# Four more seven-product units in the gate and up projections of a one-core encoder layer

## The chip, the core and the metric

The kernel runs on one core of a Trainium2 chip. The metric is the device time of one launch in microseconds. The core's engines work side by side: PE (TensorE, matrix products into PSUM), DVE (VectorE), ACT (ScalarE), POOL (GpSimd; here it issues DMAs, above all those that add into their target) and SP (SyncE; it issues most DMAs). Each takes its own instructions strictly in order.

## The reference, cut to what matters

One encoder layer over 256 tokens of width 2048: a mixing part (input projection, windowed attention, a gated recurrence, output projection), a gated feed-forward part and a gated per-layer embedding, all in fp32. The change is in the feed-forward part:

```python
fn = rms_norm(h, g_ffn_pre)                                  # 256 x 2048
ff = (silu(fn @ w_ffn_gate) * (fn @ w_ffn_up)) @ w_ffn_down  # 2048 -> 5632 -> 2048
h  = h + rms_norm(ff, g_ffn_post)
```

## The kernel before

**Tiles.** Weights come from memory in tiles of 128 partitions x 2 x 512 (512 KB): two neighbouring blocks of 128 rows, 512 columns. Every fp32 operand is split into a high part (`wh`, made by a cast on ACT at L681) and a low part (`wl` = tile minus high part, on DVE at L697); one product of a 128x128 activation block with a 128x512 weight block is then three matmuls (high-high, low-high, high-low). PE can't begin a tile before its cast, nor the third matmul on it before its low part.

**Steps.** The gate and up projections go in eleven steps f = 0 to 10, each 512 columns of both; three groups of steps (0 to 3, 4 to 7, 8 to 10) are each followed by two down steps that multiply the finished columns by `w_ffn_down`. A step takes eight *units*: one pair of row blocks (kx = 0, 2, ... 14) for both matrices, against both halves of the tokens. A plain unit is a 2x2 by 2x2 block product of eight products, 24 matmuls, on two weight tiles (L735 to L737).

**Seven-product units.** For the units kx = 0, 2, 4 of steps 2 to 10 the eight products are replaced by seven (21 matmuls, L746 to L748), as in Strassen's and Winograd's scheme. The price is paid in sums. On the side of the activations four sums `S1, S2, S7, S4` per unit are made once for all steps by `sums_of` (L847, L854, and a split at L318 and L320); their scratch space is a part of the tile `ple`, and the sums for kx = 4 go to a tile `s`. On the side of the weights each unit of each step needs three sums of 128x512 on DVE (L625, L627, L631) from the gate tile and the up tile, and one that a DMA from POOL adds in place (L650). The unit's up tile, its *second tile*, is kept from its load until late, in one of five places (`lower`, `lower2`, a part of `ple`) that are handed out in turn.

A unit's tiles are used in this order. First the *four*: four products on two tiles of sums, issued while PE is still on the step ahead. When all fours of a step are done, `made_of_four` (L794 to L803: an ACT copy, four DVE operations, an ACT copy) combines the four accumulators, and the rest of the step waits for this. Then come the plain units, between them the *two* of each unit (its kept second tile), and last the *one* (one tile for up to two units). The tables `TAKEN` and `FOURS` say after which plain unit each comes, by the kind of step: `up3` is a gate-up step with three seven-product units, `up0` one without, `down4` a down step with four.

**Order.** Everything is written in an order that a planner in the kernel makes: it holds an estimated clock per engine, costs per operation, due times and priorities (`plan.add(task, ready, late)`), and records the operations as its clocks let them start. A task added with a later ready time stands later in the queues of its engines.

**Between steps.** A step's output `mid` is transposed by DVE (L346) and sixteen small DMAs (L356, `mT<-mid`, by POOL, or half by POOL and half by SP in the last step of a group), and then cast and split for the down steps (`carried`: L318 on ACT, L320 on DVE). Partial sums of the down steps are parked in memory; the last of them come back as `mg<-part`, 1 MB for each half of the tokens (L1914, `reload`), in step 10.

Of the kernel before, what the change touches and what calls it, by code (L numbers as in the profile page):

```python
# [16 lines left out]
P = 128  # L17
# [10 lines left out]
N = 512  # L28
# [14 lines left out]
RING = 5  # L43
# [4 lines left out]
SEVEN_F = range(2, 11)  # L48

SWAPPED = [  # L50
    (lambda f: (("w_ffn_gate", f), ("w_ffn_up", f)), SEVEN_F, SEVEN_KS),
# [196 lines left out]
def layer(ctx: ExitStack, tc: tile.TileContext, a: dict, out: bass.AP):  # L248
# [211 lines left out]
    class Group:  # L460
# [50 lines left out]
        def issue(self, nxt):  # L511
# [16 lines left out]
            for i, k in enumerate(self.rest[:m]):  # L528
# [4 lines left out]
                take()  # L533
            for ch, w, n0 in self.chunks if self.apart else ():
                seg(ch, w, n0, self.lhs, self.rest[m:], first=False)
# [3 lines left out]
    TAKEN = {  # L539
        "up3": ("", "01", "2ab"), "down4": ("", "ab0", "12", "3"), "down2": ("", "01", "a"),  # L540
    }
    FOURS = {
        ("up0", "up3"): (3, 5, 7), ("up3", "up3"): (2, 3, 4), ("up3", "down4"): (2, 3, 3, 4),
# [63 lines left out]
    def sum_stream():  # L607

        for i in sorted(fours):
            at_end = i in ends_with  # L610
            for e in () if at_end else fours[i][4].values():
                yield e
# [11 lines left out]
            both = last_blocks(2)[:, 2 * j : 2 * j + 2, :] if at_end else blocks()[:, b0 : b + 1 : b - b0, :]  # L624
            nc.vector.tensor_tensor(out=both[:, 0, :], in0=Q[:, 0, :], in1=Q[:, 1, :], op=ALU.add)  # L625
            yield dve(N, take=None if at_end else f"t{j}")
            nc.vector.tensor_tensor(out=both[:, 1, :], in0=both[:, 0, :], in1=R[:, 1, :], op=ALU.add)  # L627
# [8 lines left out]
    ends_with, ends_in = {}, {}  # L636

# [121 lines left out]
    def four_products(group, j, i):  # L759
# [9 lines left out]
        product(C2.accs[0], s["S1"], i, 0, first, last)  # L769
        product(C2.accs[1], s["S2"], i, 1, first, last)  # L770
# [36 lines left out]
    def two_products(group, j, i):  # L807
# [10 lines left out]
        if i == mg1_end:  # L818
            plan.add(reload("mg", 0), plan.clk["pe"] + 15.0)
            plan.add(reload("mg", 1), plan.clk["pe"] + 23.0)  # L820
# [9 lines left out]
    def sums_of(lhs, kx, hi, lo):  # L830
# [7 lines left out]
        kind = "mid" if lhs is hP else "T4"  # L838
        for j in range(2):
            h, l = lhs.at[kx + j]  # L840
            yield dve(S, take=None if j else kind)
            if not j and lhs is hP:
# [20 lines left out]
    def more_sums():  # L863
# [5 lines left out]
        for e in hF.ev_sums.values():  # L869
            yield e  # L870
        for j in range(4):
            plan.free[f"t{j}"].append(plan.now)

# [929 lines left out]
    def up_post(f, mid, kk0, g, soon):  # L1803

        def post(ch):
# [13 lines left out]
            plan.add(carried(mid, kk0, mT), plan.now + (0.5 if soon else {0: 12.0, 9: 6.0}.get(f, 3.0)), -SOON if soon else 0.0)  # L1819
# [121 lines left out]
    for part, (f0, f1) in enumerate(PARTS):  # L1941
        mid = Mid(f"mid{part}")
        last_part = part == len(PARTS) - 1
        for f in range(f0, f1):
# [5 lines left out]
                SEVEN_KS if f in SEVEN_F else (),  # L1950
# [226 lines left out]
    for i in range(min(fours), max(f[1] for f in fours.values() if f[4] is hF.ev_sums)):  # L2177
        if i % (W_BUFS + MORE_W) < MORE_W:
            more_w[i] = i % (W_BUFS + MORE_W)
    for n, i in enumerate(sorted(lower)):  # L2180
        lower[i] = (3, 4, 0, 1, 2)[n % RING] if n < len(lower) - 2 else n + 2 - len(lower)
# [144 lines left out]
```

## Time and profile before

| | |
|---|---|
| median of 3 runs | 1143.84 us (1143.76 to 1143.87) |
| the profiled execution | 1142.69 us, span 1140.9 us, clock 0.997 |
| PE busy | 1132.0 us, 5155 instructions |
| DVE busy | 944.0 us |
| ACT busy | 732.1 us |
| POOL busy | 150.1 us |
| step 1 (396.0 to 439.5 us) | DVE busy 33.97 us of 43.5 |
| step 4 (604.5 to 646.0 us) | DVE busy 33.15 us of 41.5 |
| step 8 (852.0 to 893.5 us) | DVE busy 34.83 us of 41.5 |

All times of the trace count from the start of the span. A matmul's row lasts longer than the distance to the next one, since matmuls overlap; the distance between starts is what PE takes for one. In a row of the timeline the bracket at the end gives the idle time of the engine before the row, and what ended it.

### The profile page before, as it was taken

The page shows a single profiled execution, that of the slowest core. Times are in us where ns is not written, and L with a number is a line of the kernel's source. Part 1 is how long each engine was busy: PE and PEld are TensorE (multiplying, and loading weights), DVE is VectorE, ACT ScalarE, POOL GpSimd, SP SyncE. Part 2 cuts the span into 40 slices and gives each one's busy share as a digit, 9 for nine tenths or more (in the row PEclk, how much of TensorE's full clock was granted, in tenths as well). Part 3 has the DMA queues.
Part 4 walks back from the last instruction along what each step waited for, and adds up shares of the span by engine and source line. Part 5 has one row for each costly group of instructions (what it writes and reads, how often), then busy time and mean ns, then how long its engine had stood idle before and what let it go on. Part 6 is the DMA issues. An engine that isn't in the chain of part 4 may idle for free.

```text
span 1140.9 us, 15192 instructions
## 1 busy us (share of the span) xinstructions
PE 1132.0 (99%) x5155; PEld 940.4 (82%) x5155; DVE 944.0 (83%) x1218; ACT 732.1 (64%) x985; POOL 150.1 (13%) x240
## 2 busy tenths in 40 slices
PE   9999999999999999999999999999999999999997
PEld 7888888888888888888888888888888888888886
DVE  5768788788458778898997898999988888888886
ACT  6876788976447555666666566556564565576674
POOL 0000000000000033142110133222111313100200
PEclk9999999999999999999999999999999999999998
DMA  9867576565786996887987777897897777977863
GB/s 311 297 196 222 167 196 194 156 192 187 220 289 185 285 316 208 233 244 224 283 255 218 259 224 216 249 269 247 253 315 247 225 247 239 277 236 256 259 202 105
DMA packets 109967, 268.24 MB, mean 235 GB/s; under 512 B 36352, under 2 KB 42496, under 8 KB 108480
## 3 DMA queue, kind: packets, MB, share of 16 engines
q1 hardware_dynamic: 95568, 242.60, 64.2%
q0 software_dynamic: 14032, 24.52, 10.8%
q8 instruction: 40, 0.66, 0.2%
q14 instruction: 39, 0.32, 0.1%
q10 hardware_dynamic: 288, 0.14, 0.0%
HBM read 249.38 MB, written 9.44 MB: 227 GB/s over the span
## 4 chain that ended last, share of the span: by engine, by line
PE 97%; DMA 1%; DVE 1%; ACT 1%; issue 0%; DVEq 0%; SPq 0%; POOL 0%; ACTq 0%; POOLq 0%
PE acc L737 24%; PE acc L735 24%; PE acc L736 24%; PE acc L748 7%; PE acc L747 7%; PE acc L746 7%; PE tr L337 1%; DMA mg<-part 1%; DVE wl L697 0%; PE half L2044 0%; PE acc L2044 0%; PE warm L2227 0%; PE pg L384 0%; PE pg L385 0%; PE pg L386 0%; DMA mT<-mid 0%
## 5 line engine op out<-in xcount | busy, mean ns | idle before, releaser
L697 DVE TENSOR_TENSOR wl<-wr,wh 128x1024 fp32r<-128x1024 f32 (+1 forms) x300 | 359.2, 1209 | 96.8 <-ACT wh L681 92.1
L681 ACT CAST wh<-wr 128x1024 fp32r<-128x1024 f32 (+1 forms) x300 | 310.5, 1043 | 173.1 <-PE acc L736 115.0
L356 POOL DMA_DIRECT2D mT<-mid x164 | 96.3, 597 | 599.8 <-DMA wr<-in_w_ffn_gate 395.5
L735 PE MATMUL acc<-wh,hT_mix_hi 128*128 128x512 f32 x420 | 163.7, 390 | 0.0
L736 PE MATMUL acc<-wh,hT_mix_lo 128*128 128x512 f32 x420 | 163.5, 389 | 0.0
L737 PE MATMUL acc<-wl,hT_mix_hi 128*128 128x512 f32 x420 | 163.4, 389 | 0.0
L737 PE MATMUL acc<-wl,hT_hi 128*128 128x512 f32 x320 | 124.8, 391 | 0.0
L735 PE MATMUL acc<-wh,hT_hi 128*128 128x512 f32 x316 | 124.5, 394 | 0.0
L736 PE MATMUL acc<-wh,hT_lo 128*128 128x512 f32 x316 | 123.2, 390 | 0.0
L681 ACT CAST wh<-ple 128x1024 fp32r<-128x1024 f32 (+1 forms) x68 | 68.2, 1008 | 75.3 <-DVE ple L627 46.7
L736 PEld LDWEIGHTS acc<-wh,hT_mix_lo 128*128 128x128 f32 x420 | 78.9, 188 | 16.6 <-DVE hT_mix_lo L326 0.3
L737 PEld LDWEIGHTS acc<-wl,hT_mix_hi 128*128 128x128 f32 x420 | 78.8, 188 | 16.4
L735 PEld LDWEIGHTS acc<-wh,hT_mix_hi 128*128 128x128 f32 x420 | 78.8, 188 | 16.3 <-ACT hT_mix_hi L324 0.2
L697 DVE TENSOR_TENSOR wl<-ple,wh 128x1024 fp32r<-128x1024 f32 (+1 forms) x68 | 79.2, 1165 | 10.1 <-ACT wh L681 9.7
L737 PEld LDWEIGHTS acc<-wl,hT_hi 128*128 128x128 f32 x320 | 60.1, 188 | 13.5 <-DVE wl L697 0.6
L736 PEld LDWEIGHTS acc<-wh,hT_lo 128*128 128x128 f32 x316 | 59.4, 188 | 11.8
L735 PEld LDWEIGHTS acc<-wh,hT_hi 128*128 128x128 f32 x316 | 59.4, 188 | 11.3
L650 POOL DMA_DIRECT2D ple<-in_w_ffn_up x27 | 24.1, 891 | 167.7 <-DVE wl L697 125.1
L681 ACT CAST wh<-third 128x1024 fp32r<-128x1024 f32 x33 | 34.7, 1053 | 14.1 <-PE acc L736 8.2
L697 DVE TENSOR_TENSOR wl<-third,wh 128x1024 fp32r<-128x1024 f32 x33 | 40.2, 1220 | 0.7 <-ACT wh L681 0.5
L681 ACT CAST wh<-lower 128x1024 fp32r<-128x1024 f32 x30 | 31.4, 1051 | 13.8 <-PE acc L736 12.1
L735 PE MATMUL acc<-wh,hT_ffn_hi 128*128 128x512 f32 x96 | 37.8, 393 | 0.3 <-ACT hT_ffn_hi L324 0.3
(462 smaller groups left out, 2470.5 us busy)
## 6 DMA issues: line engine op xcount, KB each, us to landing
wr<-in_w_in SPq DMA_DIRECT2D x77, 512.0 KB, 4.4
wr<-in_w_ffn_gate SPq DMA_DIRECT2D x73, 512.0 KB, 5.4
wr<-in_w_ffn_down SPq DMA_DIRECT2D x55, 512.0 KB, 5.5
wr<-in_w_ffn_up SPq DMA_DIRECT2D x51, 512.0 KB, 4.8
wr<-in_w_out SPq DMA_DIRECT2D x32, 512.0 KB, 4.3
wr<-in_w_ple_gate SPq DMA_DIRECT2D x30, 512.0 KB, 5.3
lower<-in_w_ffn_up SPq DMA_DIRECT2D x21, 512.0 KB, 6.2
lower<-in_w_ffn_down SPq DMA_DIRECT2D x17, 512.0 KB, 5.4
```

Of the source, the lines that this page charges most:

```text
L337: nc.tensor.transpose(tr[:, b, t * P : (t + 1) * P], e[:, t, sl], ident)
L356: (nc.gpsimd if i in pool else nc.sync).dma_start(dst[32 * j : 32 * j + 32, :, :, i, :], src[32 * i : 32 * i + 32, :, :, j, :],)
L650: nc.gpsimd.dma_start(dst, src, accum_op=ALU.add)
L681: nc.scalar.copy(his[i][:, 0 : src.shape[1], :] if n == 2 else his[i][:, j, :], src)
L697: nc.vector.tensor_tensor(out=los[i][:, m, :], in0=src, in1=f32(his[i][:, m, :]), op=ALU.subtract)
L735: nc.tensor.matmul(accs[t], hi[:, sl], his[i][:, j, :], start=st, stop=False, **group)
L736: nc.tensor.matmul(accs[t], lo[:, sl], his[i][:, j, :], start=False, stop=False, **group)
L737: nc.tensor.matmul(accs[t], hi[:, sl], los[i][:, j, :], start=False, stop=sp, **group)
L746: nc.tensor.matmul(dst, x[0], wh, start=start, stop=False, skip_group_check=seeded)
L747: nc.tensor.matmul(dst, x[1], wh, start=False, stop=False, skip_group_check=seeded)
L748: nc.tensor.matmul(dst, x[0], wl, start=False, stop=stop, skip_group_check=seeded)
```

## The change

The seven-product scheme takes four more units: in step 1 the units kx = 0 and 2 (a new kind of step, `up2`), and in steps 4 and 8 also kx = 6 (kind `up4`). What comes with it:

- Step 1's two fours stand ahead of the last plain unit of step 0 (`("up0", "up2"): (7, 7)`), so that the sums for kx = 4, which must be out of the shared scratch space before any weight sum uses it, are made earlier too.
- The activation sums for kx = 6 are made later by a new task `fourth_sums`, in a `mid` tile, into a new tile `fourth`. To make room for it, `dynamic_dma_scratch_size=8192` sets the space for the descriptors of the DMAs that POOL issues; before it was left at its default.
- The places of the second tiles are handed out by longest unused, in the rotation 3, 4, 0, 1, 2, with places 0 to 2 for the last four. `flip` swaps the two blocks of a fourth unit's sums where their places would otherwise be in falling order.
- In step 10 the second half of the parked sums is planned 28 us after PE instead of 23, and the last gate-up output of each group is planned for its cast and split 2.5 us after its transposing DMAs instead of 0.5.

```diff
-RING = 5
+RING = (3, 4, 0, 1, 2)
...
-SEVEN_F = range(2, 11)
+SEVEN_F = range(1, 11)
+FOUR_F = (4, 8)
+
+
+def seven_ks(f):
+    return (0, 2, 4, 6) if f in FOUR_F else (0, 2) if f == 1 else SEVEN_KS
...
+            for j, at in enumerate(FOURS[self.kind(), nxt.kind()] if nxt and nxt.sevens else ()):
+                if at >= n:
+                    nxt.four(j)
...
     TAKEN = {
+        "up2": ("", "0", "1a"),
+        "up4": ("", "ab0", "1", "23"),
         "up3": ("", "01", "2ab"), "down4": ("", "ab0", "12", "3"), "down2": ("", "01", "a"),
     }
     FOURS = {
+        ("up0", "up2"): (7, 7), ("up2", "up3"): (2, 3, 4),
+        ("up3", "up4"): (2, 3, 3, 4), ("up4", "up3"): (1, 2, 3), ...
...
-            for e in () if at_end else fours[i][4].values():
-                yield e
+            for e in () if at_end else fours[i][4].items():
+                if e[0] != 6 or fours[i][4] is not hF.ev_sums or fours[i][2] == 3:
+                    yield e[1]
...
+    def flip(i, j):
+        return int(i not in ends_with and j == 3 and first_slot[i] == 0)
...
-            plan.add(reload("mg", 1), plan.clk["pe"] + 23.0)
+            plan.add(reload("mg", 1), plan.clk["pe"] + 28.0)
...
-        kind = "mid" if lhs is hP else "T4"
+        kind = "mid" if lhs is hP or kx == 6 else "T4"
...
+        plan.add(fourth_sums(), plan.now + 20.0, LATE)
+
+    def fourth_sums():
+        pair = t2["pool"].tile([P, 2, N], F32R, name="fourth")
+        yield from sums_of(hF, 6, pair[:, 0, :], pair[:, 1, :])
...
-            plan.add(carried(mid, kk0, mT), plan.now + (0.5 if soon else {0: 12.0, 9: 6.0}.get(f, 3.0)), -SOON if soon else 0.0)
+            plan.add(carried(mid, kk0, mT), plan.now + (2.5 if soon else {0: 12.0, 9: 6.0}.get(f, 3.0)), -SOON if soon else 0.0)
...
-                SEVEN_KS if f in SEVEN_F else (),
+                seven_ks(f) if f in SEVEN_F else (),
...
-        lower[i] = (3, 4, 0, 1, 2)[n % RING] if n < len(lower) - 2 else n + 2 - len(lower)
+        lower[i] = next(j for j in places if j < 3 or n < len(lower) - 4)
+        places.remove(lower[i])
+        places.append(lower[i])
...
-    nc = bacc.Bacc("TRN2", target_bir_lowering=False, num_devices=1)
+    nc = bacc.Bacc("TRN2", target_bir_lowering=False, num_devices=1, dynamic_dma_scratch_size=8192)
```

PE's program falls from 5144 to 5132 instructions, DVE's rises from 1218 to 1246, ACT's from 930 to 938 and POOL's from 245 to 249; SP has 567 in both. Up to the fourteenth weight tile of step 0 the order is the same on every engine. In the rows below, a line number of the changed kernel is 6 to 24 higher than that of the same statement before: L715 is L697, L326 is L320, L332 is L326, L866 is L847, L873 is L854, L640, L642 and L646 are L625, L627 and L631, L699 is L681, L324 is L318, L362 is L356, L584 is L571 and L1938 is L1914.

**DVE at the end of step 0.** `hT_mix_lo` is the low part of the activations' last four blocks, `s` the activation sums for kx = 4, `ple<-wr` and the rows like it weight sums. Before, in the order of the program:

```order
L326 SCALAR_TENSOR_TENSOR hT_mix_lo<-mT,vec,hT_mix_hi 128x256 x4
L847 TENSOR_TENSOR ple<-hT_mix_hi,hT_mix_lo 128x256
L697 TENSOR_TENSOR wl<-wr,wh 128x1024
L847 TENSOR_TENSOR ple<-hT_mix_hi,hT_mix_lo 128x256
L697 TENSOR_TENSOR wl<-wr,wh 128x1024
L854 TENSOR_TENSOR ple<-ple 128x128
L697 TENSOR_TENSOR wl<-wr,wh 128x1024
L854 TENSOR_TENSOR ple<-ple 128x128
L697 TENSOR_TENSOR wl<-wr,wh 128x1024
```

And now, from the same row on:

```order
L332 SCALAR_TENSOR_TENSOR hT_mix_lo<-mT,vec,hT_mix_hi 128x256 x4
L866 TENSOR_TENSOR ple<-hT_mix_hi,hT_mix_lo 128x256 x2
L873 TENSOR_TENSOR ple<-ple 128x128 x4
L326 TENSOR_TENSOR s<-ple,s 128x512
L640 TENSOR_TENSOR ple<-wr 128x512
L642 TENSOR_TENSOR ple<-ple,lower_3577 128x512
L646 TENSOR_TENSOR wr<-wr,lower_3577 128x512
L640 TENSOR_TENSOR ple<-wr 128x512
L715 TENSOR_TENSOR wl<-ple,wh 128x1024
L642 TENSOR_TENSOR ple<-ple,lower_3577 128x512
L715 TENSOR_TENSOR wl<-wr,wh 128x1024
L646 TENSOR_TENSOR wr<-wr,lower_3577 128x512
```

The next three rows are `w<-ple,w`, and `wl<-wr,wh` three times. The low parts of four tiles stood between the activation sums; now the sums for kx = 4 and four of the six weight sums of step 1 stand together ahead of the first low part of step 1's fours.

**ACT at the first down step after step 10.** `mid2h` is the cast of step 10's output, which waits for the DMAs `mT<-mid`. Before:

```order
L681 CAST wh<-lower 128x1024
L681 CAST wh<-ple 128x1024
L681 CAST wh<-third 128x1024
L681 CAST wh<-wr 128x1024
L681 CAST wh<-ple 128x1024
L318 CAST mid2h_8487<-mT 128x512
L681 CAST wh<-ple 128x1024
L318 CAST mid2h_8487<-mT 128x512
```

Now:

```order
L699 CAST wh<-lower 128x1024 x2
L699 CAST wh<-wr 128x1024
L699 CAST wh<-third 128x1024
L699 CAST wh<-ple 128x1024 x2
L324 CAST mid2h_8506<-mT 128x512
L699 CAST wh<-wr 128x1024
L324 CAST mid2h_8506<-mT 128x512
```

One more weight cast stands ahead of the first `mid2h`.

**SP at the same place.** Before, the second half of the parked sums stood ahead of the transposing DMAs:

```order
L571 DMA wr<-in_w_ffn_down 128x1024 x2
L1914 DMA mg_8424<-part_100 128x2048
L356 DMA mT<-mid 32x8x32 x8
L571 DMA third<-in_w_ffn_down 128x1024
L571 DMA lower<-in_w_ffn_down 128x1024
```

Now it stands behind them and behind three weight loads:

```order
L584 DMA wr<-in_w_ffn_down 128x1024 x2
L362 DMA mT<-mid 32x8x32 x8
L584 DMA wr<-in_w_ffn_down 128x1024
L584 DMA lower<-in_w_ffn_down 128x1024
L584 DMA third<-in_w_ffn_down 128x1024
L1938 DMA mg_8529<-part_100 128x2048
```

More of the change, by code (lines that the diff above doesn't have):

```diff
@@ L47 @@
 OUT = (3, 6, 7, 1)
-SEVEN_F = range(2, 11)
+SEVEN_F = range(1, 11)
+FOUR_F = (4, 8)
+def seven_ks(f):
+    return (0, 2, 4, 6) if f in FOUR_F else (0, 2) if f == 1 else SEVEN_KS
 SWAPPED = [
-    (lambda f: (("w_ffn_gate", f), ("w_ffn_up", f)), SEVEN_F, SEVEN_KS),
+    *((lambda f: (("w_ffn_gate", f), ("w_ffn_up", f)), (f,), seven_ks(f)) for f in SEVEN_F),
     *(
@@ L623, in sum_stream @@
             yield dve(N, take=None if at_end else f"T{n}")
-            both = last_blocks(2)[:, 2 * j : 2 * j + 2, :] if at_end else blocks()[:, b0 : b + 1 : b - b0, :]
-            nc.vector.tensor_tensor(out=both[:, 0, :], in0=Q[:, 0, :], in1=Q[:, 1, :], op=ALU.add)
+            both = last_blocks(2)[:, 2 * j : 2 * j + 2, :] if at_end else blocks()[:, min(b, b0) : max(b, b0) + 1 : abs(b - b0), :]
+            z = flip(i, j)
+            nc.vector.tensor_tensor(out=both[:, z, :], in0=Q[:, 0, :], in1=Q[:, 1, :], op=ALU.add)
             yield dve(N, take=None if at_end else f"t{j}")
-            nc.vector.tensor_tensor(out=both[:, 1, :], in0=both[:, 0, :], in1=R[:, 1, :], op=ALU.add)
+            nc.vector.tensor_tensor(out=both[:, 1 - z, :], in0=both[:, z, :], in1=R[:, 1, :], op=ALU.add)
             raws[i] = both
@@ L768, in four_products @@
         s = group.lhs.sums[kx]
-        product(C2.accs[0], s["S1"], i, 0, first, last)
-        product(C2.accs[1], s["S2"], i, 1, first, last)
+        z = flip(i, j)
+        product(C2.accs[0], s["S1"], i, z, first, last)
+        product(C2.accs[1], s["S2"], i, 1 - z, first, last)
         spent(i)
@@ L841, in sums_of @@
             yield dve(S, take=None if j else kind)
-            if not j and lhs is hP:
+            if not j and kind == "mid":
                 at_ = mid_tile()
@@ L868, in more_sums @@
         yield from sums_of(hF, 4, t2["s"][:, 0, :], t2["s"][:, 1, :])
-        for e in hF.ev_sums.values():
-            yield e
+        for kx in SEVEN_KS:
+            yield hF.ev_sums[kx]
         for j in range(4):
             plan.free[f"t{j}"].append(plan.now)
+        plan.add(fourth_sums(), plan.now + 20.0, LATE)
+    def fourth_sums():
+        pair = t2["pool"].tile([P, 2, N], F32R, name="fourth")
+        yield from sums_of(hF, 6, pair[:, 0, :], pair[:, 1, :])
     ev_unmerged = Event()
@@ L2179, in layer @@
             more_w[i] = i % (W_BUFS + MORE_W)
+    places = list(RING)
     for n, i in enumerate(sorted(lower)):
-        lower[i] = (3, 4, 0, 1, 2)[n % RING] if n < len(lower) - 2 else n + 2 - len(lower)
+        lower[i] = next(j for j in places if j < 3 or n < len(lower) - 4)
+        places.remove(lower[i])
+        places.append(lower[i])
     first_slot = {i: n % 2 for n, i in enumerate(sorted(fours))}
```

1 row of the table FOURS is left out of this document.

## The prediction

> **What bounds the kernel now.** I read the page first: busy time, then the chain that ended last.
>
> ```profile
> span 1140.9 us, 15192 instructions
> PE 1132.0 (99%) x5155; PEld 940.4 (82%) x5155; DVE 944.0 (83%) x1218; ACT 732.1 (64%) x985; POOL 150.1 (13%) x240
> PE 97%; DMA 1%; DVE 1%; ACT 1%; issue 0%; DVEq 0%; SPq 0%; POOL 0%; ACTq 0%; POOLq 0%
> ```
>
> PE is busy for all but 8.9 us and makes 97% of the chain. Next, the windows over most of the gate and up steps and over the three steps that change (time; then busy time of PE, weight loads, DVE, ACT, POOL; granted clock; DMA share; GB/s):
>
> ```profile
> 400.00:970.00 570.00, 570.00 (x2517) 472.12 (x2516) 502.99 (x558) 338.93 (x369) 130.88 (x198) 1.00 0.80 249
> 396.00:439.50 43.50, 43.50 (x193) 36.05 (x192) 33.97 (x37) 22.07 (x23) 12.29 (x19) 1.00 0.91 289
> 604.50:646.00 41.50, 41.50 (x184) 34.36 (x183) 33.15 (x35) 24.47 (x28) 4.16 (x5) 1.00 0.79 251
> 852.00:893.50 41.50, 41.50 (x184) 34.38 (x184) 34.83 (x39) 22.37 (x24) 4.10 (x5) 1.00 0.81 272
> ```
>
> For 570 us PE has no gap, at full clock, so in the steps that change nothing but the number of matmuls sets the time, as long as the tiles come early enough. What decides the sum is therefore (a) what a matmul takes, (b) where PE waits now and whether the change touches it, (c) where the change makes PE wait.
>
> **The change: matmuls.** PE's timeline over one plain weight tile of step 0 (start, duration as recorded, line):
>
> ```profile
> 387.84 0.39 PE L735 MATMUL acc<-wh,hT_mix_hi 128*128 128x512 f32 x1
> 388.30 0.39 PE L737 MATMUL acc<-wl,hT_mix_hi 128*128 128x512 f32 x1
> 390.56 0.39 PE L735 MATMUL acc<-wh,hT_mix_hi 128*128 128x512 f32 x1
> ```
>
> From the first row to the last the tile's twelve matmuls pass: 2.72 us, 0.2267 each. Each new seven-product unit does 21 matmuls in place of 24. Four units make twelve fewer: **−2.72 us**, all on the path while PE has no gap. The bounds are narrow, since PE's matmuls of both kinds stand at this distance.
>
> By the Trainium skill ("TensorE: Matmul & The Clock Gate", section "Back-to-back issue gap") a sustained stream of matmuls with 512 columns runs at about 131 ns each. By that the twelve would be worth 1.57 us and the time would come out 1.15 us higher, at 1142.3; the trace's 226.7 ns doesn't agree.
>
> **The stall that may go.** In the first down step after step 10 PE does wait:
>
> ```profile
> 993.72 0.39 PE L746 MATMUL acc<-wh,sums 128*128 128x512 f32 x1
> 995.98 0.50 PE L748 MATMUL acc<-wl,mid2h 128*128 128x512 f32 x1
> 996.32 0.39 PE L746 MATMUL acc<-wh,sums 128*128 128x512 f32 x1
> ```
>
> From the first row's start to the last one's nine matmuls are issued. At 0.2267 us they would take 2.04 us; they took 2.60, so **0.56 us** is lost there. Where it comes from, the chain of waits over this stretch tells:
>
> ```profile
> 978.98 8.86 DMA mg<-part
> 987.85 3.41 DMA mT<-mid
> 994.71 1.23 DVE wl L697
> 995.98 0.50 PE acc L748
> ```
>
> PE waits for a low part that DVE made late. Up the chain stand the transposed blocks `mT` of step 10's output, and ahead of them the 1-MB load of the parked sums. ACT shows it from the other side, and SP the order of issue, here beside the same move in an earlier step that has no such load:
>
> ```profile
> 978.98 0.43 SPq L1914 DMA_DIRECT2D mg<-part  x1
> 981.20 7.23 SPq L356 DMA_DIRECT2D mT<-mid  x8
> 991.36 0.62 ACT L318 CAST mid2h<-mT 128x512 fp32r<-128x512 f32 x1 [4.77 <-DMA mT<-mid]
> ...
> 532.97 5.18 SPq L356 DMA_DIRECT2D mT<-mid  x8
> 541.17 0.62 ACT L318 CAST mid0h<-mT 128x512 fp32r<-128x512 f32 x1 [1.34 <-DMA mT<-mid]
> ```
>
> ACT stood 4.77 us before the first `mid2h`, with the weight casts queued behind it, and DVE's low parts behind those. The cast came 10.16 us after the first issue with the load ahead, and 8.20 us without it. In the new order the load stands behind the eight transfers and three weight loads, and one more weight cast (1.05 us) stands ahead of `mid2h`. I take the 1.96 us of earlier data for what the load's new place is worth; with the cast that is 3.0 of ACT's 4.77 us, and five times the 0.56 that PE lost. So the stall goes: **−0.56 us**. The bounds are 0, if the data come no earlier, and −0.56; more than was lost can't be won. What is late next is the load itself: its sums are added in the last down step, far behind, and I cost it at nothing. If it now took bandwidth from weight loads, those would pay (a rival below).
>
> **A new knot at step 1's fours.** Here the change queues more ahead of the first low part that PE needs. The rows that price it:
>
> ```profile
> 378.46 1.23 DVE L697 TENSOR_TENSOR wl<-wr,wh 128x1024 fp32r<-128x1024 f32 x1 [0.52 <-ACT wh L681]
> 379.60 1.67 DVE L326 SCALAR_TENSOR_TENSOR hT_mix_lo<-mT,vec,hT_mix_hi 128x256 fp32r<-128x256 f32 x4
> 363.05 0.76 DVE L847 TENSOR_TENSOR ple<-hT_mix_hi,hT_mix_lo 128x256 f32<-128x256 f32 x2
> 365.14 1.02 DVE L854 TENSOR_TENSOR ple<-ple 128x128 f32<-128x128 f32 x4
> 391.49 0.62 ACT L318 CAST s<-ple 128x512 fp32r<-128x512 f32 x1
> 458.09 0.68 DVE L625 TENSOR_TENSOR ple<-wr 128x512 f32<-128x512 f32 x1
> 458.81 0.69 DVE L627 TENSOR_TENSOR ple<-ple 128x512 f32<-128x512 f32 x1
> 399.82 1.23 DVE L697 TENSOR_TENSOR wl<-wr,wh 128x1024 fp32r<-128x1024 f32 x1
> 400.97 0.69 DVE L627 TENSOR_TENSOR ple<-ple,lower 128x512 f32<-128x512 f32 x1
> 401.57 0.68 DVE L631 TENSOR_TENSOR wr<-wr,lower 128x512 f32<-128x512 f32 x1
> 401.76 1.05 ACT L681 CAST wh<-ple 128x1024 fp32r<-128x1024 f32 x1 [1.97 <-DVE ple L627]
> ```
>
> Starts next to each other give what an operation costs in a queue: a 128x512 sum 0.60 us (400.97 to 401.57), L625's 0.72 (458.09 to 458.81), a low part 1.15 (399.82 to 400.97) and 1.23 to its end. Up to `hT_mix_lo` nothing differs, so that group ends at 379.60 + 1.67 = 381.27 as before. From there, in the new order on DVE: the additions, 0.76, and the second ones, 1.02: 383.05. ACT casts `s`, 0.62: 383.67. The split of `s`, 0.60, and the first weight sum, 0.72: 385.0. The second, 0.60: 385.6; now ACT can cast the first tile of sums, 1.05, until 386.7. Meanwhile DVE does two more sums, 0.60 and 0.72, to 386.9. Then the four low parts with two sums between them: first from 386.9 to 388.1 (1.15 to the next start), a sum to 388.7, second to 389.9 (next start 389.8), a sum to 390.4, third to 391.7, fourth to 392.8.
>
> PE reaches this place at 387.84 as before. A tile of a four has six matmuls, 1.36 us, and needs its low part at the third: 388.30, 389.66, 391.02, 392.38. The first is in time by 0.2. The second is 0.24 late, which moves the next need to 391.26; the third is then 0.4 late, the next need 393.0, and the fourth is in time. That makes **+0.6 us**. Bounds: 0, since 0.7 us less on the way from `s` to the third low part (an early start of the sums, whose tiles don't depend on `s`) undoes it; and about +1.5, if two waits of 0.5 for a cast, as the row at 378.46 shows one, come in between, because DVE and ACT hand each other work five times here. I take the sum of the rows.
>
> **The work that hides.** A new unit costs DVE three sums and half again as many low parts (3.5 tiles instead of 2): 3 x 0.60 + 1.5 x 1.15 = 3.5 us. Steps 4 and 8 have 41.5 − 33.15 = 8.35 and 41.5 − 34.83 = 6.67 us of idle DVE, so one unit fits each. In step 1 DVE is idle for 43.5 − 33.97 = 9.5 us; the new units' sums and fours stand ahead of the step, so what comes into it is mainly the combination of the accumulators,
>
> ```profile
> 439.66 0.69 DVE L796 TENSOR_TENSOR u<-u,acc 128x512 f32<-128x512 f32 x1 [0.53 <-ACT u L794]
> ```
>
> four times 0.69 = 2.8 us, and the sums of `fourth`, 0.76 + 1.02 + 0.60 = 2.4: 5.2 of 9.5. What counts beside the average is how early a low part is at its narrowest. Before, the narrowest that cost nothing was
>
> ```profile
> 463.51 1.22 DVE L697 TENSOR_TENSOR wl<-wr,wh 128x1024 fp32r<-128x1024 f32 x1
> 465.14 0.39 PE L737 MATMUL acc<-wl,hT_mix_hi 128*128 128x512 f32 x1
> ```
>
> ready at 464.73, used at 465.14: 0.41 us. Carrying DVE's new order forward against PE's with the durations above, I estimate that behind the knot the low parts stay 0.7 us or more ahead, lowest around 455 to 463 where a step's move and the sums meet as before. So I put the DVE and ACT work elsewhere at nothing, the weight traffic too (the units load the same tiles), and the reordered places of the second tiles.
>
> **Sum.** −2.72 − 0.56 + 0.6 = −2.7 us. The profiled execution took 1142.69 us (its span is 1140.9) and is 1.15 below the median of the three timed runs, 1143.84. On its own time the sum gives 1140.0, on the timed basis **1141.1 us**. A measurement of this kernel can tell about 0.2% from no change, 2.3 us, so faster means below 1141.55.
>
> **The rivals.**
>
> No knot: DVE starts step 1's sums early, and PE has no new gap. For it speaks that the sums read only loaded tiles; against it, that the order puts `s` ahead of them in DVE's queue. −3.28: 1140.5 us. Chance 0.10.
>
> A longer knot, 1.0 to 2.0 us, in the same place or with a second one where step 1's combination meets the next sums. For it: every hand-over between ACT and DVE in this chain is counted without a pause, and the first low part has 0.2 us to spare. 1141.6 to 1142.6. Chance 0.18.
>
> The stall stays or moves: behind the transfers, the 8.86-us load runs beside the weight loads of the down step, a tile comes late, and ACT waits for that instead of `mT`. For it: the load lasted 8.9 us and three tiles of the down step are issued just ahead of it; against it: those three are ahead. −2.72 + 0.6: 1141.7. Chance 0.12.
>
> A removed matmul is worth less than its distance. Were PE's rate set by weight loads or by sequencing at some other place, twelve fewer could give half, 1.4 us: 1142.4. Against it stand 570 us without a gap, the loads busy for 472 of them. Chance 0.03.
>
> Slower: POOL's transfers run short of descriptor space.
>
> ```profile
> 447.56 8.16 POOL L356 DMA_DIRECT2D mT<-mid  x14 [14.07 <-DVE mid L346]
> 456.75 0.58 POOL L356 DMA_DIRECT2D mT<-mid  x1 [1.03 <-DMA mT<-mid]
> 462.26 0.61 ACT L318 CAST mid0h<-mT 128x512 fp32r<-128x512 f32 x1
> mT<-mid POOLq DMA_DIRECT2D x164, 32.0 KB, 5.0
> ```
>
> POOL issues a transfer in 0.58 us and each lands 5.0 us later, so some eight are under way at once; in the program each of POOL's DMAs already waits for the one eight before it, as at 456.75. If the smaller space holds only four, sixteen take four rounds of 5.0 + 0.58 = 22.3 us in place of the 10.9 from 447.56 to 458.4. The cast at 462.26 would be 11 us late, and the low part behind it was used 0.41 us after its end, so some 11 us reach PE in this move alone: 1152 us or more. It decides from the point where fewer than eight 32-KB transfers fit. Against it: eight are half of a move's sixteen, and the space is halved, not cut to a fourth. Chance 0.07.
>
> The Trainium skill ("DMA: Bandwidth & Descriptors", section "SWDGE vs HWDGE vs iDMA") says that GpSimd writes the descriptors of its DMAs into rings in SBUF, which an engine drains. No run here shows how many fit.
>
> **How the numbers follow.** The forecast has 0.50. Faster is the forecast and no knot, 0.60; within 0.2% the longer knot, the stall that stays, and the cheap matmul, 0.33; slower 0.07. The range goes from no knot with 0.2 below it for the spread of the runs, 1140.3, to a stall that stays and a knot at its bound (1143.84 − 2.72 + 1.5 = 1142.6) with 0.2 above it, 1142.8.
>
> **What would show it.** PE at 0.227 us between starts, with twelve rows fewer. A gap of PE before third matmuls between 388 and 392, 0.6 us in all, with wl behind weight sums in the chain of waits; none there means no knot. No wait of PE around 991 to 994, and ACT's idle time before the first `mid2h` down from 4.77 to about 2 us; if ACT waits as long for `mT` or for a weight tile, the stall has only moved. POOL's issues still 0.58 us each in rows of fourteen or so; pauses after every few would be the descriptor space. I am wrong if PE shows a gap of a microsecond in steps 1 to 9 behind the knot, since then DVE's narrowest lead was judged too well.

## The result, and the profile after

| | before | after |
|---|---|---|
| median of 11 runs each | 1143.56 us (1143.11 to 1144.95) | 1140.74 us (1140.15 to 1142.03) |
| ratio, 95% interval | | 0.9976 (0.9968 to 0.9984) |
| the profiled execution | 1142.69 us | 1142.03 us |

The change makes the kernel 2.8 us faster by the medians (1.8 to 3.7 by the interval). The profiled execution of the changed kernel is the slowest of its eleven, so the two pages are 0.7 us apart, not 2.8. The page after, its first lines and the chain:

```profile
span 1140.2 us, 15230 instructions
PE 1129.4 (99%) x5143; PEld 939.1 (82%) x5143; DVE 960.7 (84%) x1246; ACT 739.7 (65%) x993; POOL 153.3 (13%) x244
PE 90%; DVE 4%; DMA 3%; ACT 2%; issue 1%; SPq 0%; DVEq 0%; POOL 0%; ACTq 0%; POOLq 0%
```

PE has twelve rows fewer and 2.6 us less to do. Its share of the chain fell from 97% to 90%, but that is not 7% of waiting: where PE waits once, the chain goes back through what it waited for, and all that came before on that other path counts as DVE, DMA or ACT. Where PE waits is seen in its timeline. At step 1's fours (start, duration, line):

```profile
388.84 0.39 PE L764 MATMUL acc<-wh,at_hi 128*128 128x512 f32 x1
...
390.49 0.40 PE L765 MATMUL acc<-wh,hT_mix_lo 128*128 128x512 f32 x1
390.98 0.51 PE L766 MATMUL acc<-wl,hT_mix_hi 128*128 128x512 f32 x1
391.32 0.40 PE L764 MATMUL acc<-wh,at_hi 128*128 128x512 f32 x1
...
392.71 0.50 PE L766 MATMUL acc<-w,sf 128*128 128x512 f32 x1
...
395.12 0.39 PE L753 MATMUL acc<-wh,hT_mix_hi 128*128 128x512 f32 x1
```

The 24 matmuls of the two fours begin at 388.84 and the next plain tile at 395.12: 6.28 us for 24 x 0.2267 = 5.44. So 0.84 us is lost, in front of third matmuls, those that need a low part. DVE's rows say why:

```profile
380.66 1.67 DVE L332 SCALAR_TENSOR_TENSOR hT_mix_lo<-mT,vec,hT_mix_hi 128x256 fp32r<-128x256 f32 x4
384.74 0.69 DVE L326 TENSOR_TENSOR s<-ple,s 128x512 fp32r<-128x512 f32 x1 [0.69 <-ACT s L324]
389.70 1.22 DVE L715 TENSOR_TENSOR wl<-wr,wh 128x1024 fp32r<-128x1024 f32 x1
391.44 1.22 DVE L715 TENSOR_TENSOR w<-ple,w 128x1024 fp32r<-128x1024 f32 x1
```

DVE works almost without a pause (one of 0.69 us, for ACT's cast of `s`) and ends the second and the third low part at 390.92 and 392.66, just ahead of the two late matmuls. At the other place, the first down step after step 10, ACT and SP show that the stall of before is gone:

```profile
980.32 5.45 SPq L362 DMA_DIRECT2D mT<-mid  x8
987.40 0.43 SPq L1938 DMA_DIRECT2D mg<-part  x1
988.75 0.61 ACT L324 CAST mid2h<-mT 128x512 fp32r<-128x512 f32 x1
```

The 1-MB load is issued behind the transfers, and the cast waits for nothing (no bracket), 8.43 us after the first issue. ACT's pause now stands one row ahead, before the added weight cast, which waits for a sum by DVE:

```profile
987.80 1.05 ACT L699 CAST wh<-ple 128x1024 fp32r<-128x1024 f32 x1 [2.09 <-DVE ple L642]
```

In the steps that gained work, DVE came nearer to its limit and PE still has no gap:

```profile
395.00:436.00 41.00, 41.00 (x183) 33.96 (x182) 38.34 (x48) 26.16 (x30) 12.09 (x19) 1.00 0.85 274
602.00:643.00 41.00, 41.00 (x183) 33.98 (x182) 34.20 (x36) 26.35 (x29) 4.16 (x5) 1.00 0.83 257
849.00:890.00 41.00, 41.00 (x183) 33.97 (x182) 36.42 (x40) 24.01 (x25) 5.75 (x8) 1.00 0.86 280
```

**A measure for the experiments.** Timed runs of one kernel lie 1 to 3 us apart, so a half microsecond must be read from traces. Apart from the matmuls removed, all kernels here do the same work from one matmul in the middle of step 0 to the last one of the down steps; before and after:

```profile
352.34 0.48 PE L735 MATMUL acc<-wh,hT_mix_hi 128*128 128x512 f32 x1
...
1041.68 0.39 PE L737 MATMUL acc<-wl,pTh 128*128 128x512 f32 x1
```

```profile
353.33 0.48 PE L753 MATMUL acc<-wh,hT_mix_hi 128*128 128x512 f32 x1
...
1040.21 0.39 PE L755 MATMUL acc<-wl,pTh 128*128 128x512 f32 x1
```

That is 689.34 us before and 686.88 after, 2.46 less. The changed kernel's first row is a microsecond later although its program is the same up to there, which is one reason why its profiled execution was slow; another stands in the last section.

### The profile page after: what moved, and what is told of

Same layout as the page of the kernel before. It is cut to its first block, busy times and chain, and to the rows that moved or that the text cites. A ratio compares the mean times of both kernels' runs of the same rounds, so it can differ in the third digit from the quotient of the medians.

```text
span 1140.2 us, 15230 instructions
## 1 busy us (share of the span) xinstructions
PE 1129.4 (99%) x5143; PEld 939.1 (82%) x5143; DVE 960.7 (84%) x1246; ACT 739.7 (65%) x993; POOL 153.3 (13%) x244
## 4 chain that ended last, share of the span: by engine, by line
PE 90%; DVE 4%; DMA 3%; ACT 2%; issue 1%; SPq 0%; DVEq 0%; POOL 0%; ACTq 0%; POOLq 0%
PE acc L755 22%; PE acc L754 21%; PE acc L753 21%; PE acc L766 7%; PE acc L765 7%; PE acc L764 7%; DVE wl L715 1%; DMA wr<-in_w_ffn_up 1%; DMA h<-h_spill 1%; PE tr L343 1%; ACT wh L699 1%; DVE h L1652 0%; DVE hT_mix_lo L332 0%; DMA sq<-ev 0%; PE half L2068 0%
## 5 line engine op out<-in xcount | busy, mean ns | idle before, releaser
L715 DVE TENSOR_TENSOR wl<-wr,wh 128x1024 fp32r<-128x1024 f32 (+1 forms) x296 | 354.3, 1210 | 75.9 <-ACT wh L699 69.1
L699 ACT CAST wh<-wr 128x1024 fp32r<-128x1024 f32 (+1 forms) x296 | 306.2, 1043 | 150.2 <-PE acc L754 93.1
L753 PE MATMUL acc<-wh,hT_mix_hi 128*128 128x512 f32 x388 | 151.5, 390 | 0.0
L754 PE MATMUL acc<-wh,hT_mix_lo 128*128 128x512 f32 x388 | 151.3, 390 | 0.0
L755 PE MATMUL acc<-wl,hT_mix_hi 128*128 128x512 f32 x388 | 151.2, 390 | 0.0
L362 POOL DMA_DIRECT2D mT<-mid x164 | 95.9, 605 | 228.5 <-DVE mid L352 111.2
L699 ACT CAST wh<-ple 128x1024 fp32r<-128x1024 f32 (+1 forms) x72 | 72.9, 1017 | 81.2 <-DVE ple L642 48.6
L668 POOL DMA_DIRECT2D ple<-in_w_ffn_up x31 | 27.7, 893 | 542.7 <-DVE ple L642 387.6
L715 DVE TENSOR_TENSOR wl<-ple,wh 128x1024 fp32r<-128x1024 f32 (+1 forms) x72 | 84.4, 1176 | 9.0 <-ACT wh L699 8.9
L754 PEld LDWEIGHTS acc<-wh,hT_mix_lo 128*128 128x128 f32 x388 | 72.9, 188 | 15.3 <-DVE hT_mix_lo L332 0.3
L753 PEld LDWEIGHTS acc<-wh,hT_mix_hi 128*128 128x128 f32 x388 | 72.9, 188 | 15.2 <-ACT hT_mix_hi L330 0.2
L755 PEld LDWEIGHTS acc<-wl,hT_mix_hi 128*128 128x128 f32 x388 | 72.9, 188 | 15.1
L699 ACT CAST wh<-lower 128x1024 fp32r<-128x1024 f32 x34 | 35.6, 1051 | 13.5 <-PE acc L754 9.6
L699 ACT CAST wh<-third 128x1024 fp32r<-128x1024 f32 x31 | 32.6, 1052 | 17.4 <-PE acc L754 10.7
L715 DVE TENSOR_TENSOR wl<-third,wh 128x1024 fp32r<-128x1024 f32 x31 | 37.9, 1222 | 5.5 <-ACT wh L699 5.1
L715 DVE TENSOR_TENSOR wl<-lower,wh 128x1024 fp32r<-128x1024 f32 x34 | 41.1, 1217 | 0.0
```

The lines of the kernel that those rows point to most:

```text
L362: (nc.gpsimd if i in pool else nc.sync).dma_start(dst[32 * j : 32 * j + 32, :, :, i, :], src[32 * i : 32 * i + 32, :, :, j, :],)
L668: nc.gpsimd.dma_start(dst, src, accum_op=ALU.add)
L699: nc.scalar.copy(his[i][:, 0 : src.shape[1], :] if n == 2 else his[i][:, j, :], src)
L715: nc.vector.tensor_tensor(out=los[i][:, m, :], in0=src, in1=f32(his[i][:, m, :]), op=ALU.subtract)
L753: nc.tensor.matmul(accs[t], hi[:, sl], his[i][:, j, :], start=st, stop=False, **group)
L754: nc.tensor.matmul(accs[t], lo[:, sl], his[i][:, j, :], start=False, stop=False, **group)
```

## The experiments

The stretch of every trace, and what it lost: its length less that of the kernel that loses nothing (the third row), corrected by 0.2267 us per matmul removed. Each ratio is to the kernel before, timed in the same rounds. The rows without a median are of kernels that ran once, for their trace: 1143.58, 1141.78, 1142.42, 1156.17 and 1140.49 us in the order of the table.

| kernel | matmuls | stretch, us | lost, us | where | timed median, us (ratio, interval) |
|---|---|---|---|---|---|
| before | 0 | 689.34 | 0.61 | down step after step 10 | 1143.56 |
| before, second trace | 0 | 689.86 | 1.13 | same | |
| before, the two new times | 0 | 688.73 | 0 | | |
| changed | −12 | 686.88 | 0.87 | step 1's fours | 1140.74 (0.9976, 0.9968 to 0.9984) |
| changed, second trace | −12 | 686.43 | 0.42 | same | 1141.20 (0.9977, 0.9968 to 0.9986) |
| changed, old times | −12 | 686.43 | 0.42 | same | 1141.72 (0.9985, 0.9976 to 0.9993) |
| changed, load at 23 us | −12 | 687.92 | 1.91 | fours 0.40, down step 1.5 | |
| changed, no units in step 1 | −6 | 687.39 | 0.02 | | 1141.42 (0.9982, 0.9973 to 0.9991) |
| changed, first unit's sums ahead | −12 | 688.57 | 2.56 | step 1's fours | 1141.42 (0.9981, 0.9972 to 0.9989) |
| changed, blocks split earlier | −12 | 687.86 | 1.85 | same | 1141.90 (0.9986, 0.9977 to 0.9996) |
| changed, one row moved | −12 | 686.07 | 0.06 | | 1140.98 (0.9979, 0.9968 to 0.9989) |
| that, with a unit in step 6 | −15 | 691.87 | 6.54 | steps 6 and 7 | 1145.40 (1.0014, 1.0004 to 1.0024) |
| changed, units in 4 to 10 | −27 | 702.59 | 20.0 | steps 5 to 10, down steps | |
| changed, descriptor space 2048 | −12 | 686.44 | 0.43 | step 1's fours | |

### The changed kernel again

> The changed kernel a second time, as the base for the others on the same chip. Theory: twelve matmuls fewer (-2.72 us), the stall at the first down step after step 10 gone (-0.56), a knot of 0.8 us before the low parts of step 1's fours, so about -2.5 to -2.8 us against before. The knot must show again, with the same size within 0.2 us, if it comes from DVE's order. The first profile has besides a wait of PE for h, behind its reload from memory, at 1041 us, 0.56 us more than before; if the change made it, it shows again, and if it is one execution's slow transfer, it doesn't.

The knot is there again, but half as large, which is outside the 0.2 us that the expectation allowed: the fours begin at 387.75 and the next plain tile at 393.58, 5.83 us, so 0.39 is lost.

```profile
379.12 1.67 DVE L332 SCALAR_TENSOR_TENSOR hT_mix_lo<-mT,vec,hT_mix_hi 128x256 fp32r<-128x256 f32 x4
387.75 0.39 PE L764 MATMUL acc<-wh,at_hi 128*128 128x512 f32 x1
391.17 0.50 PE L766 MATMUL acc<-w,sf 128*128 128x512 f32 x1
```

DVE begins its chain 8.63 us ahead of PE here and 8.18 us ahead (380.66 to 388.84) in the first trace: 0.45 more, and 0.45 less is lost. In the first trace ACT made the high parts late, since it stood 1.06 us for a weight load ahead of them:

```profile
378.43 1.05 ACT L699 CAST wh<-wr 128x1024 fp32r<-128x1024 f32 x1 [1.06 <-DMA wr<-in_w_ffn_up]
```

In the second trace the same cast waits for a matmul of PE instead:

```profile
376.89 1.05 ACT L699 CAST wh<-wr 128x1024 fp32r<-128x1024 f32 x1 [0.83 <-PE acc L754]
```

So the chain's length is set by the order, and the knot is what that length exceeds the lead. Where this cast waits for PE the lead is always the same: it is 8.63 or 8.64 us in this trace and in those of three kernels below with the same order here (old times, load at 23 us, descriptor space 2048), and 0.40 to 0.43 us is lost in each. A late load shortens the lead, as in the first trace; its 0.84 is the exception and 0.4 the usual size.

### The first unit's sums ahead

```diff
-        for e in () if at_end else fours[i][4].items():
-            if e[0] != 6 or ...
+            if (i > min(fours) or not e[0]) and (e[0] != 6 or ...)
...
-        done(ev_unmerged)
+        plan.free["t0"].append(plan.now)
         yield from sums_of(hF, 4, t2["s"][:, 0, :], t2["s"][:, 1, :])
...
+        done(ev_unmerged) if sub is mix else None
```

The last line stands in `next_norm`, behind the last use of `mg`; the three other places of sums are handed out as before.

> The changed kernel, with the weight sums of step 1's first unit planned as soon as its tiles are there: they no longer wait for the activation sums of kx = 4, whose scratch they don't touch. Theory (the knot is DVE's order): the first two low parts of the fours are ready over a microsecond earlier, PE has no gap from 388 to 393 us, and the time is 0.8 us under the changed kernel, 3.3 to 3.6 under before. Rival (the tiles come late, whatever the order): DVE waits for the loads in the new place, the gaps stay, and the time is that of the changed kernel.

Both theories fell. The loads are there, the first unit's low parts come over 2 us earlier, and the loss is three to six times larger:

```profile
391.02 0.39 PE L766 MATMUL acc<-wl,at_hi 128*128 128x512 f32 x1
392.84 0.50 PE L764 MATMUL acc<-w,sf 128*128 128x512 f32 x1 [1.43 <-ACT w L699]
394.11 0.50 PE L766 MATMUL acc<-w,sf 128*128 128x512 f32 x1 [0.53 <-DVE w L715]
```

What was put ahead for the first unit stands in front of the second one's chain: the second additions, `s`, its weight sums, its cast. PE now waits even for the high part. The chain to look at ends with the third low part, not with the first. Its timed median is only 0.2 us over that of the second trace's kernel, and the profiled execution (1142.52 us) is the slowest of its eleven, so this trace may show more than an average execution loses; that is open.

### The blocks split earlier

```diff
-plan.add(split_turned(c, mT, hi, lo, nxt, gname), plan.now + (LATER if nxt is hP else 0.0), -SOON)
+plan.add(split_turned(c, mT, hi, lo, nxt, gname), plan.now + (LATER if nxt is hP else -2.0), -SOON if nxt is hP else -4 * SOON)
```

> The changed kernel with the last four blocks of the activations planned 2 us earlier and ahead of others, so that their high parts stand on ACT in front of the casts of step 0's last tiles, which wait for loads, and their low parts on DVE in front of the last activation sums. Theory (the knot is the length of the chain from these blocks to the third low part, some 10.4 us on DVE with its one pause): the chain starts 1 us or more earlier and the knot of 0.34 to 0.8 us goes, with nothing else changed: 0.3 to 0.8 us under the changed kernel. Rival (the blocks' transfers land only then): ACT waits for them, the casts behind come late, and the knot stays or grows.

The rival is right. The transfers of these blocks land no earlier because they are planned earlier, and ACT, now without a cast ahead to fill the time, stands for them:

```profile
377.84 1.71 ACT L330 ACTIVATE hT_mix_hi<-mT,vec 128x256 fp32r<-128x256 f32 x4 [2.51 <-DMA mT<-mid]
```

The low part of step 0's last tile and the split of `sf` were thereby pushed behind, into the chain, and 1.85 us was lost.

### One row moved

```diff
-                    yield e[1]
+                    yield ev_subs if i == min(fours) and e[0] == 4 else e[1]
...
+        done(ev_subs) if lhs is hF and kx == 4 else None
         yield from split(hi, lo, f, N, give=kind)
```

The second line stands behind the four subtractions of `sums_of`; `ev_unmerged` is set earlier as above. On DVE only the first `L640` moves, ahead of the split of `s`.

> The changed kernel with one DVE row of the chain moved: the first weight sum of step 1 stands in the 0.69-us pause in which DVE waits for ACT's cast of the activation sums for kx = 4. Theory (the knot is the length of that chain): the third low part comes 0.6 to 0.7 us earlier and the knot of 0.34 to 0.8 us shrinks to 0 to 0.1. Rival (something else holds the low parts): the knot stays, as it did when unit 1's sums were moved wholly ahead or the blocks were split earlier.

```profile
383.78 0.69 DVE L640 TENSOR_TENSOR ple<-wr 128x512 f32<-128x512 f32 x1
384.55 0.69 DVE L326 TENSOR_TENSOR s<-ple,s 128x512 fp32r<-128x512 f32 x1
390.52 1.22 DVE L715 TENSOR_TENSOR w<-ple,w 128x1024 fp32r<-128x1024 f32 x1
```

The pause is filled and the third low part starts 10.05 us after `hT_mix_lo` (380.47), against 10.78 in the changed kernel (380.66 to 391.44): 0.73 less. PE has no gap there, and 0.06 us is lost in the whole stretch. The lead is 8.36 us (380.47 to 388.83), between those of the two traces of the changed kernel that lost 0.84 and 0.39, so it isn't a longer lead that took the knot away. So the knot is the length of this chain on DVE. As a kernel it is worth 0.4 to 0.8 us in the traces, and nothing that its timed median can tell from the changed kernel's.

### Without step 1's units

```diff
-SEVEN_F = range(1, 11)
+SEVEN_F = range(2, 11)
```

> The changed kernel without step 1's two units: that step is a plain one as before, steps 4 and 8 keep four units. Theory: six matmuls more than the changed kernel (+1.36 us) and no knot (-0.8): 0.56 us over it, 2.0 us under before, and no gap of PE around 388 us. Rival (the two units cost more than their knot, by a full DVE in steps 1 and 2): equal to the changed kernel or faster.

Six matmuls come back (1.36 us), nothing is lost at step 1, and the stretch is 0.96 longer than that of the second trace and 0.51 longer than that of the first. So in the traces these two units gain, and their knot is their whole price: DVE in steps 1 and 2 costs nothing more. The timed medians, 1141.42 and 1141.20 in the same rounds, are too close to tell.

### The two planned times

```diff
-            plan.add(reload("mg", 1), plan.clk["pe"] + 28.0)
+            plan.add(reload("mg", 1), plan.clk["pe"] + 23.0)
...
-... plan.now + (2.5 if soon else ...
+... plan.now + (0.5 if soon else ...
```

> The changed kernel with the two planned times of before: the second half of the parked sums 23 us after PE and the last output's cast 0.5 us behind its transfers. Theory: the 1-MB load stands ahead of the transposing transfers again, ACT waits some 4 to 5 us before the first cast of step 10's output, PE loses 0.5 to 0.6 us at the start of that down step, and the time is 0.56 us over the changed kernel. Rival (the stall went because the new fourth units shifted the tiles): no gap there, same time as the changed kernel.

There is no gap, against the theory: the load stands ahead of the transfers, but the data come 9.40 us after the first issue and not 10.16.

```profile
979.40 6.51 SPq L362 DMA_DIRECT2D mT<-mid  x8
988.80 0.62 ACT L324 CAST mid2h<-mT 128x512 fp32r<-128x512 f32 x1 [4.00 <-DMA mT<-mid]
```

Two more runs were to tell whether the fourth units or the load had removed the stall. First the kernel before once more:

> The kernel before a second time, for its trace alone: is the 0.56-us stall at the first down step after step 10 there in every execution? The changed kernel with the old planned times had none, with ACT waiting 4.0 us for the transposed blocks instead of 4.77. Theory now: the stall sits on a margin of a few tenths of a microsecond, and is there when the transfers behind the 1-MB load land 0.6 us or more later than in that run; then this trace has either ACT waiting under 4.3 us and no gap, or over 4.5 and a gap. Rival (the fourth units shifted the tiles): ACT waits as before, 4.8 us, and the gap of 0.5 to 0.6 us is there.

```profile
981.64 8.09 SPq L356 DMA_DIRECT2D mT<-mid  x8
992.33 0.62 ACT L318 CAST mid2h<-mT 128x512 fp32r<-128x512 f32 x1 [5.29 <-DMA mT<-mid]
995.21 0.50 PE L748 MATMUL acc<-wl,sums 128*128 128x512 f32 x1 [0.41 <-DVE wl L697]
```

10.69 us after the first issue, and 1.13 us lost. With the same order on ACT the three traces are 9.40, 10.16 and 10.69 us, with 0, 0.6 and 1.1 lost: what lies beyond about 9.6 is lost. Then the kernel before with nothing but the two new times (28 and 2.5):

> The kernel before with the two planned times of the change alone: the second half of the parked sums planned 28 us after PE, the last output's cast 2.5 us behind its transfers. It has the same matmuls as before. Theory (the load's place makes the stall): the 1-MB load stands behind the transposing transfers, ACT waits at most 2.5 us before the first cast of step 10's output, and PE has no gap at the start of that down step, where the two traces of before lost 0.56 and 1.02 us with ACT waiting 4.77 and 5.29. Rival (the fourth units' shift of the tiles removed it, as the changed kernel with the old planned times, which had no stall, suggests): the gap is still there, 0.5 us or more.

```profile
980.97 5.44 SPq L356 DMA_DIRECT2D mT<-mid  x8
988.05 0.43 SPq L1914 DMA_DIRECT2D mg<-part  x1
989.42 0.61 ACT L318 CAST mid2h<-mT 128x512 fp32r<-128x512 f32 x1
```

The cast has no wait and PE no gap, without a single new unit, so the two new times removed the stall and not the fourth units. What the load does to the transfers is seen in all these traces: the eight `mT<-mid` of SP land 5.5 to 6.4 us after their issue in the median where the load stands ahead of them (both traces of before, the old times, the next run), and 2.0 to 2.5 us in the ten others, where it stands behind. Then the load alone put back, with the cast left at 2.5:

> The changed kernel with the load of the parked sums alone put back to 23 us; the cast stays at 2.5. The load then stands ahead of the transposing transfers again. Theory (a margin): PE loses what ACT waits beyond some 4.2 us less the 1.05 of the cast that now stands ahead of it; with the data 9.4 to 10.7 us after the first issue, as in the three traces with the load ahead, ACT waits 2 to 4 us and PE loses nothing or a few tenths. Rival (the load's place alone decides): the data come 9.4 us or later and PE loses 0.5 us or more.

```profile
979.81 8.25 SPq L362 DMA_DIRECT2D mT<-mid  x8
990.23 0.62 ACT L324 CAST mid2h<-mT 128x512 fp32r<-128x512 f32 x1 [0.91 <-DMA mT<-mid]
995.08 0.50 PE L766 MATMUL acc<-wl,mid2h 128*128 128x512 f32 x1 [0.78 <-DVE wl L715]
```

The rival is right: the data come 10.42 us after the first issue. ACT waits only 0.91, since casts stand ahead, and PE yet loses 1.5 us, more than with the old times together. The later cast fills ACT's wait and moves what PE needs behind `mid2h` further back: on DVE the low part that PE waits for starts at 993.81, behind both low parts of `mid2h` and a weight sum, where it stands between those two low parts in the changed kernel (990.63). Whether the kernel with both old times loses nothing in other executions too is open; its timed median is 0.5 us over that of the changed kernel in the same rounds, within the intervals. Nor does any run have the load behind the transfers and the cast at 0.5, so what the later cast is worth by itself isn't shown.

### More fourth units

```diff
-FOUR_F = (4, 8)
+FOUR_F = (4, 5, 6, 7, 8, 9, 10)
```

> The changed kernel with a fourth unit in all steps from 4 to 10, five more than it has: 15 matmuls fewer, 3.4 us by the distance between matmuls, and 3.5 us more of DVE's work in each of these steps. Theory (a step's DVE has room for one more unit as long as 6 us and more were idle): no new gap of PE over 0.3 us except where a move and the sums meet; 1137.5 to 1138.5. Rival (neighbouring steps with four units leave DVE no time to get ahead again): gaps of a microsecond or more in steps 5 to 10, and no gain over the changed kernel.

The gaps that the rival forecast are there, and 20 us are lost, from step 5 on. Its reason isn't seen at the first of them, where DVE is not full (35.0 of 41 us; in the 41 us behind, 37.9); ACT stands for a move:

```profile
643.00:684.00 41.00, 39.93 (x175) 32.25 (x174) 35.02 (x41) 22.14 (x25) 11.65 (x19) 1.00 0.66 205
671.94 0.62 ACT L324 CAST mid1h<-mT 128x512 fp32r<-128x512 f32 x1 [3.72 <-DMA mT<-mid]
```

With one such step, 6, between steps with three units, on the kernel with the moved row:

> The kernel with the moved row, and a fourth unit in step 6 too: three matmuls fewer, -0.68 us. In the run with fourth units in all of steps 4 to 10 PE lost 16 us in the steps with a move of the output to the down steps' form, first behind an ACT wait of 3.7 us for such a move, while DVE was idle for 6 of 41 us. Theory (it is the moves and not DVE's load): step 6, which has a move, loses a microsecond or more at its fours even between steps with three, and the time is over the changed kernel's. Rival (neighbouring steps with four units are the trouble): no gap, 0.7 us under the kernel with the moved row.

```profile
697.07 7.01 POOL L362 DMA_DIRECT2D mT<-mid  x12 [12.96 <-DVE mid L352]
713.93 0.62 ACT L324 CAST mid1h<-mT 128x512 fp32r<-128x512 f32 x1 [8.82 <-DMA mT<-mid]
715.55 0.50 PE L764 MATMUL acc<-wh,sf 128*128 128x512 f32 x1 [1.79 <-ACT wh L699]
```

ACT stands 8.8 us for the transposed output with weight casts behind it, and PE after it. A neighbour with four units isn't needed: one more unit in a step with a move is enough. POOL's order differs too: the 256-KB DMA that adds into one of the weight sums (L668, L650 before) now stands ahead of the last four of the sixteen transfers,

```profile
704.08 0.98 POOL L668 DMA_DIRECT2D ple<-in_w_ffn_up  x1
706.43 7.40 DMA mT<-mid
```

and these four land 7.4 to 7.6 us after their issue. In the kernel with the moved row alone that DMA comes behind all sixteen (707.03), and the last two land after 1.8 us. The run with units in 4 to 10 has the same order at its first gap, and 7.0 to 7.5 us for the last four. So it looks like the parked sums again, a larger transfer ahead of small ones; but SP's weight loads run at the same time, and no run moves this DMA alone. Steps 4 and 8 have no move of sixteen (POOL is busy for 4.2 and 5.8 us of 41 above, against 11.7 in step 5). DVE has no pause at the first of the gaps in this run (a low part at 696, 0.8 us lost): there PE waits for DVE's own queue, and its load plays a part.

### A fourth of the descriptor space

```diff
-    nc = bacc.Bacc(..., dynamic_dma_scratch_size=8192)
+    nc = bacc.Bacc(..., dynamic_dma_scratch_size=2048)
```

> The changed kernel with a fourth of its descriptor space, 2048 in place of 8192. Theory: eight transfers of POOL at once, which the program itself allows, still fit, so POOL issues in 0.58 us each as before and the time is that of the changed kernel; with 8192 the size then had a wide margin. Rival (space is what limits POOL): its issues pause, the moves of 16 take 15 us and more, and PE waits behind them; over 1145 us.

```profile
447.49 5.31 POOL L362 DMA_DIRECT2D mT<-mid  x9 [18.62 <-DVE mid L352]
453.16 2.33 POOL L362 DMA_DIRECT2D mT<-mid  x4 [0.36 <-issue]
```

POOL now pauses where the profile shows nothing that it waits for (0.36 us behind the ninth issue, then 1.18 and 0.89), the move of sixteen takes 12.3 us instead of 11.3 in the changed kernel and 10.9 before, and nothing is lost by it: the stretch is that of the changed kernel's second trace. The time came as the theory has it, though the issues don't run on quite as before; whether the pauses are the space is open. 8192 is four times the size that does this.

## Why the prediction was right, point by point

It forecast 1141.1 us with a sum of −2.7 us; the medians differ by 2.8, and the new one lies at 1140.74.

- **Twelve matmuls, −2.72.** Right. The two kernels that lose nothing, the one before with the new times and the one with the moved row, differ by 688.73 − 686.07 = 2.66 us, 0.222 a matmul; the 0.06 that the table calls lost in the second is the rest to 2.72 and not a measured wait. The rival of a cheaper matmul, at 1.4 us, is out.
- **The stall, −0.56.** The mechanism is right: the 1-MB load ahead of the transfers. Its size was taken from one execution, and a second trace has 1.1, and a kernel with the same order none. It is a margin that the transfers overrun by more or less. Ten traces have both new times, and PE waits there in one of them only, that with a fourth unit in all of steps 4 to 10. The forecast of ACT's idle time was about 2 us, and 2.09 is left, but one row earlier and for DVE. The 1.05 us that was credited to the added weight cast isn't shown: with the load in its old place the later cast came with a loss of 1.5 us, where another weight cast stood ahead of `mid2h` besides.
- **The knot, +0.6.** Right in place, mechanism and about in size: 0.84 and 0.39 by the fours' timeline. The chain was forecast to end the third low part 12.1 us after the start of `hT_mix_lo` (379.60 to 391.7), and it ended after 12.0. That the size fits the first trace is in part luck: the lead was taken from a trace of before in which the same load was late (387.84 − 379.60 = 8.24), and with the usual lead of 8.63 the same sum gives about 0.3. Missing from the sum was a cost after each wait: the next matmul comes 0.34 us behind the late one and not 0.2267 (390.98 to 391.32). The prediction's own rows at 995.98 and 996.32 already show it. The lower bound's reason was wrong. An early start of the first unit's sums didn't undo the knot but made it 2.5 us; what undoes it is the filled pause.
- **The work that hides.** Right that no other place stalls: no trace of the changed kernel has a new gap in steps 1 to 10. The idle time left to DVE in step 1 was put at 4.3 of 43.5 us and is 2.7 of 41. (3.5 low parts instead of 2 are three quarters more and not half; the sum used the right 1.5.)
- **Descriptor space.** That rival needed fewer than eight transfers to fit; even with a fourth of the new size POOL issued nine before its first pause.

The errors of the terms reach about half a microsecond each and partly cancel: in some executions more stall is removed than forecast or the knot is larger, in others less. The interval of the timed runs, 1.8 to 3.7 us, can't tell such terms apart. So the matmuls and both mechanisms are shown by the traces, while a total within 0.1 us is luck.

## What to carry to other kernels

Where an engine is busy all the time, an edit's gain is the work it removes, and its risk lies where the order puts new work ahead of a tile that is needed next: add up that queue row by row, to the last tile of the group, and look for a pause in it that another row can fill. Putting one unit's work first moves the next unit's wait, and planning an operation ahead of its data turns a fillable pause into a standing engine. In two places here small transfers were late behind a larger one (in the first shown, in the second likely): look for that order in every queue that issues DMAs. A stall seen in one trace may be a margin: look at a second execution before its size goes into a sum.

## What the runs showed of the hardware

**A long pause of PE cost more than its length.** In the kernel with a unit in step 6, after PE stood from 713.37 to 716.80 but for two matmuls, the next ones came at nearly twice the distance:

```profile
716.80 0.64 PE L766 MATMUL acc<-wl,sf 128*128 128x512 f32 x1 [0.52 <-DVE wl L715]
717.24 0.63 PE L764 MATMUL acc<-wh,sf 128*128 128x512 f32 x1
```

0.43 us in place of 0.2267, for eight intervals, some 1.6 us more. The granted clock from 716.8 to 720.2 was 0.53. In the kernel with units in 4 to 10 a stand of 3.82 us, counted from start to start with the two matmuls in it, did the same (the one here is 3.43), and two of 2.93 and 2.99 us didn't, nor did one of 3.09 us in the kernel with the first unit's sums ahead. The Trainium skill ("TensorE: Matmul & The Clock Gate", section "What's actually happening") says that the array's clock is halved after an idle window of about 3.4 us that runs freely. The distance agrees (1.9 times), and so do the lengths if the two matmuls don't make the window a busy one, which no run here shows.

**One 1-MB load was late in one execution.** In the first trace of the changed kernel the second half of `h` came back late, and PE, which had not waited for it before, did:

```profile
1029.53 9.76 DMA h<-h_spill
1041.78 0.55 PE L343 MATMUL tr<-ident,h 128*128 128x128 f32 x3 [0.62 <-DVE h L1652]
```

Its issue stands 10.68 us ahead of the last matmul of the down steps in both first traces (1031.00 to 1041.68 before, 1029.53 to 1040.21 after), and no other trace of the changed kernel has the wait. The load took 9.76 us to land, against 5.6 to 8.4 in eleven other traces, and 0.56 us was lost by it. It is one execution's slow transfer, and not part of the change.
